# Dilated attention: exchanging the softmax statistics of two set layouts on chip, and scaling the second set on ScalarE

## The chip, the core and the metric

The kernel runs on one core of one Trainium2 chip. The metric is the device time of one execution in microseconds; the median of three runs before the change is 2357.65 us (2355.96 to 2360.38). Engines are named as the profile names them: PE is TensorE's matmul, PEld its weight load, DVE is VectorE, ACT is ScalarE, POOL is GpSimd, SP is SyncE, which only issues DMAs here.

## The reference, cut to what matters

Eight layers follow each other on 512 tokens of width 1024: a dilated attention ("dil"), a differential attention ("diff"), a recurrent mixer, cross attentions, MLPs and a sliding-window attention, each with a norm before and after. The change lies in the first one. For each of 16 heads there are three groups of queries, keys and values with (window, dilation) of (128, 1), (512, 4) and (2048, 16); each group has its own softmax over its own keys, and the three outputs are mixed by a softmax over the groups' log-denominators:

```python
    outs, lses = [], []
    for g, (window, dil) in enumerate(DIL_GROUPS):
        sl = slice(g * DIL_HEADS, (g + 1) * DIL_HEADS)
        o, lse = dilated_window_attention(q[:, :, sl], k[:, :, sl], v[:, :, sl], window, dil)
        outs.append(o)
        lses.append(lse)
    alpha = jax.nn.softmax(jnp.stack(lses, axis=0), axis=0)
    o = jnp.sum(alpha[..., None] * jnp.stack(outs, axis=0), axis=0)
    y = o.reshape(B, S, DIL_WIDTH).astype(h.dtype) * jax.nn.silu(gate)
    return y @ w_out
```

That mixing is the same as one softmax over the scores of all three groups together, for each query.

## The kernel before, in words

Matrix products in fp32 are made of three products of split operands (`mm3`, L364 to L372): an ACT instruction rounds a weight half to `whi` (L443), a DVE instruction takes the rest `wlo` (L444), and each pair of operands takes three matmuls (L370, L371, L372). A projection of 128 columns over 512 tokens (`unit`, L395) is 24 such matmuls into a PSUM tile `pj`.

The dilated stage (`dil`, L817) goes through eight pairs of heads (hp). For each pair it projects queries and keys of the three groups (`proj`, two units of 24 matmuls for each group), rotates them on DVE (L601) and POOL (L603), and lays them out as `qk` by DMAs of 32 partitions (L614, on the SP queue). While hp is projected, PE is also given the attention of the pair before: `plan` (L921) puts 18 steps of the generator `attend` (L830) into a list, and `fm` calls the next step between the matmuls of a unit, after its third and its sixth of eight pairs (`self.cuts = 3, 6`) and at its end. Six units with three calls each take the 18 steps of one pair. For the last pair (hp 7) two steps are taken at each call (`self.rate = 2`, L941).

The steps of one pair:

- Steps 0 to 3: scores of set 0 (group 0, queries in an order where partition p of tile i belongs to one block of 128 tokens), and their softmax part: a DVE instruction takes mask, scale and the negative maximum (L632), an ACT instruction the exponential with its sum (L634). Unnormalised weights go to `pa`, maximum and sum to `st[0]` [128 partitions, 4 tiles, 2 heads, 2 values].
- Steps 4 to 6: the same for set 1 (groups 1 and 2 share one softmax of 256 columns, tokens sorted by their residue mod 4) into `pb` and `st[1]`.
- Still in step 6: `merge(st)` (L953) and the scaling of `pa` and `pb` (L870).
- Steps 7 to 12 do nothing (`for _ in range(7): yield`, L872).
- Steps 13 to 17: `turn` transposes `pa` and `pb` on PE (L886), copies the result from PSUM to `PT` on ACT (L279) and DVE (L277), and `weigh` multiplies by the values (L900) into one PSUM tile `pv`; the first `turn` is that of `pa`.

In `merge` each set needs the other set's maximum and sum of the same query, which lies in another partition and another tile: query (partition 32 n + l, tile m) of one set is (partition 32 m + l, tile n) of the other. Before the change each `st` is written to a DRAM tile `ds` by one DMA (L960 for set 0, L961 for set 1) and read back in the other layout by four DMAs each (L965 into `ot[1]`, L966 into `ot[0]`), ten DMAs for each pair of heads on the SP queue. Then for each set nine small instructions on tiles of 8 columns form the factor `f` (DVE L973 to L975, ACT exponential L976, DVE L977 to L981), and 16 DVE instructions of up to 128x256 scale the weights (L870).

The order of each engine's queue is not the order of the source: the framework sorts the instructions when the kernel is built, giving each engine the earliest instruction of the source whose operands it reckons ready by then. On the chip each queue is then worked off strictly in that order, an instruction waits where its operands are late, and all behind it wait too. SP's queue holds the weight loads (L301), the `qk` moves (L614) and the ten DMAs of `merge`.

Of the kernel before, what the change touches and what calls it, by code (L numbers as in the profile page):

```python
# [12 lines left out]
F32 = mybir.dt.float32  # L13
F32R = mybir.dt.float32r
I32 = mybir.dt.int32
AF = mybir.ActivationFunctionType
ALU = mybir.AluOpType
# [3 lines left out]
S = 512  # L21
# [192 lines left out]
class Prog:  # L214
# [602 lines left out]
    def dil(self):  # L817
        nc = self.nc
        y = []
        self.v_phase("dil")  # L820
        with self.vg, self.pool("rt_dil") as rp, self.pool("dl") as p:
# [3 lines left out]
            v, gates, qk, sm = {}, self.gates, {}, {}  # L825
# [4 lines left out]
            def attend(hp):  # L830
                pa, pb = (p.tile([P, NT, 2, 256], F32, tag="p", name=n, bufs=2) for n in ("pa", "pb"))
                st = [self.sm.tile([P, 4, 2, 2], F32, tag=f"st{s}", name=f"st{s}", bufs=2) for s in range(2)]
                q0, q1, q2 = (qk.pop((hp, g)) for g in range(3))
                for i in range(NT):
                    lo = 0 if i else P
# [29 lines left out]
                f = self.merge(st)  # L865
                for s, pp in enumerate((pa, pb)):
                    for i in range(NT):
                        for h in range(2):
                            lo = P if s == 0 and i == 0 else 0
                            nc.vector.tensor_scalar(out=pp[:, i, h, lo:256], in0=pp[:, i, h, lo:256],  # L870
                                                    scalar1=f[s][:, i, h:h + 1], scalar2=None, op0=ALU.mult)
                for _ in range(7):  # L872
                    yield
                o = self.ps("pv")
# [46 lines left out]
            def plan(hp):  # L921

                it = attend(hp)

                def step(n):
                    next(it, None)
                    if n == 6 and hp:
                        gated(hp - 1)

                self.steps_between += [partial(step, n) for n in range(18)]  # L930
# [22 lines left out]
    def merge(self, st):  # L953

        nc = self.nc

        d = [self.dr.tile([S, 4], F32, tag=f"ds{s}", name=f"ds{s}", bufs=2) for s in range(2)]
        ot = [self.sm.tile([P, 4, 2, 2], F32, tag=f"ot{s}", name=f"ot{s}", bufs=2) for s in range(2)]
        st2, ot2 = ([t.rearrange("p i h c -> p i (h c)") for t in z] for z in (st, ot))
        nc.sync.dma_start(out=d[0].rearrange("(p i) c -> p i c", i=4), in_=st2[0])  # L960
        nc.sync.dma_start(out=d[1].rearrange("(r p) c -> p r c", r=4), in_=st2[1])  # L961
        of0, of1 = d[0].rearrange("(r l i) c -> i l r c", r=4, i=4), d[1].rearrange("(r i l) c -> r l i c", r=4, i=4)
        for n in range(4):
            ns = slice(32 * n, 32 * (n + 1))
            nc.sync.dma_start(out=ot2[1][ns], in_=of0[n])  # L965
            nc.sync.dma_start(out=ot2[0][ns], in_=of1[n])  # L966
        res = []
        for s in range(2):
            a, b = st[s], ot[s]
            e = self.sm.tile([P, 2, 4, 2], F32, tag="me", name="me", bufs=2)  # L970
            n = self.sm.tile([P, 4, 2], F32, tag="mn", name="mn", bufs=2)
            f = self.sm.tile([P, 4, 2], F32, tag=f"mf{s}", name=f"mf{s}", bufs=2)
            nc.vector.tensor_tensor(out=n, in0=a[:, :, :, 0], in1=b[:, :, :, 0], op=ALU.min)  # L973
            nc.vector.tensor_tensor(out=e[:, 0], in0=n, in1=a[:, :, :, 0], op=ALU.subtract)
            nc.vector.tensor_tensor(out=e[:, 1], in0=n, in1=b[:, :, :, 0], op=ALU.subtract)  # L975
            nc.scalar.activation(out=e, in_=e, func=AF.Exp)  # L976
            nc.vector.tensor_tensor(out=n, in0=e[:, 0], in1=a[:, :, :, 1], op=ALU.mult)  # L977
            nc.vector.tensor_tensor(out=f, in0=e[:, 1], in1=b[:, :, :, 1], op=ALU.mult)
            nc.vector.tensor_tensor(out=n, in0=n, in1=f, op=ALU.add)
            nc.vector.reciprocal(out=n, in_=n)  # L980
            nc.vector.tensor_tensor(out=f, in0=e[:, 0], in1=n, op=ALU.mult)  # L981
            res.append(f)
        return res
# [819 lines left out]
```

## Time and profile before

| What | Value |
|---|---|
| Median of three runs | 2357.65 us |
| The profiled execution's own time | 2357.28 us |
| Its span, first to last instruction | 2355.5 us |
| Mean granted TensorE clock | 0.997 of 2.4 GHz |
| Busy: PE, PEld | 2297.0 us (98%), 1872.4 us (79%) |
| Busy: DVE, ACT, POOL | 1429.9 us (61%), 1090.3 us (46%), 745.8 us (32%) |

The busy time of an engine is the union of its instructions' times; where it is short of the span, the engine was idle. The profile's views name for each idle stretch the releaser, what ended it. A timeline row merges neighbouring instructions of one form and shows in brackets the idle time in front of it. Attention of the dilated stage runs from about 209 to 610 us; its windows here are 195 to 640 us.

### The profile page before, as it was taken

The numbers are of one execution on the slowest core, as the hardware profiler recorded it, in microseconds if no ns is written. First come the engines' busy times: TensorE is split into PE (matmuls) and PEld (weight loads), VectorE is DVE, ScalarE is ACT, GpSimd is POOL, SyncE is SP. The second block draws the span as 40 slices with busy tenths as digits, with TensorE's granted clock in tenths as the row PEclk, the third lists the DMA queues.
The fourth block names the chain that finished last, engine by engine and source line by source line (L and its number), as shares of the span: only waits on it lengthen the run. The fifth ranks groups of instructions, "written<-read, shape, count | busy, mean of one in ns | idle before, by whom it ended". The sixth has DMA issues, their size and how long they took to land.

```text
span 2355.5 us, 33109 instructions
## 1 busy us (share of the span) xinstructions
PE 2297.0 (98%) x12168; PEld 1872.4 (79%) x12168; DVE 1429.9 (61%) x2458; ACT 1090.3 (46%) x2145; POOL 745.8 (32%) x799
## 2 busy tenths in 40 slices
PE   7999999999999999999999999999999999999998
PEld 6887777767788877878898888887966988888887
DVE  7664665666565555765655544468777744644476
ACT  4443333334344444544444454457456533544464
POOL 5962211211122222100300276671211200577640
PEclk9999999999999999999999999999999999999999
DMA  6335443333332222222442355556332332455555
GB/s 232 130 122 154 118 119 93 108 97 82 123 117 90 90 81 93 84 72 73 133 162 72 108 179 197 197 178 215 133 99 89 127 126 72 144 189 191 195 204 168
DMA packets 115874, 309.51 MB, mean 131 GB/s; under 512 B 28940, under 2 KB 35116, under 8 KB 115712
## 3 DMA queue, kind: packets, MB, share of 16 engines
q1 hardware_dynamic: 114912, 305.46, 39.2%
q0 software_dynamic: 800, 1.94, 0.3%
q8 instruction: 96, 1.57, 0.3%
q14 instruction: 66, 0.54, 0.1%
HBM read 253.72 MB, written 33.69 MB: 122 GB/s over the span
## 4 chain that ended last, share of the span: by engine, by line
PE 60%; DVE 4%; POOL 3%; ACT 2%; issue 2%; DMA 1%; SPq 0%; POOLq 0%; DVEq 0%; ACTq 0%
PE pj L370 13%; PE pj L371 13%; PE pj L372 13%; PE sc L370 3%; PE sc L371 3%; PE sc L372 3%; DVE wlo L444 1%; PE pv L370 1%; PE pv L372 1%; PE pv L371 1%; PE sc L1659 1%; PE sc L1024 1%; DVE h L521 1%; POOL quad L354 1%; PE pt L491 1%
## 5 line engine op out<-in xcount | busy, mean ns | idle before, releaser
L444 DVE TENSOR_TENSOR wlo<-raw,whi 128x1024 fp32r<-128x1024 f32 x348 | 445.3, 1286 | 329.6 <-ACT whi L443 317.2
L370 PE MATMUL pj<-uh,whi 128*128 128x512 f32 (+1 forms) x1424 | 561.9, 395 | 0.2 <-ACT ho L1350 0.2
L372 PE MATMUL pj<-uh,wlo 128*128 128x512 f32 (+1 forms) x1424 | 553.7, 389 | 2.1 <-DVE wlo L444 2.1
L371 PE MATMUL pj<-ul,whi 128*128 128x512 f32 (+1 forms) x1424 | 554.2, 389 | 0.0
L443 ACT ACTIVATE whi<-raw 128x1024 fp32r<-128x1024 f32 x348 | 365.7, 1057 | 394.1 <-PE pj L371 162.3
L354 POOL TENSOR_TENSOR quad<-quad 128x256 f32<-128x256 f32 x352 | 347.0, 1022 | 83.0 <-DVE wlo L444 37.9
L370 PEld LDWEIGHTS pj<-uh,whi 128*128 128x128 f32 x1424 | 268.0, 188 | 71.2 <-issue 15.9
L372 PEld LDWEIGHTS pj<-uh,wlo 128*128 128x128 f32 x1424 | 268.0, 188 | 60.1 <-issue 4.0
L371 PEld LDWEIGHTS pj<-ul,whi 128*128 128x128 f32 x1424 | 268.7, 189 | 54.2 <-issue 4.8
L603 POOL TENSOR_TENSOR ro<-rt 128x512 f32<-128x512 f32 x74 | 127.5, 1735 | 534.9 <-DVE rt L601 366.5
L466 POOL TENSOR_SCALAR rs<-ss 128x1 f32<-128x1 f32 x32 | 23.9, 747 | 540.6 <-ACT bq L512 540.3
L444 DVE TENSOR_TENSOR wlo<-quad,whi 128x1024 fp32r<-128x1024 f32 x90 | 124.8, 1390 | 75.7 <-ACT whi L443 75.6
L370 PE MATMUL sc<-whi,yh 128*128 128x512 f32 x384 | 151.3, 394 | 2.9 <-DVE acc L1524 2.9
L371 PE MATMUL sc<-wlo,yh 128*128 128x512 f32 x384 | 150.8, 393 | 1.0 <-DVE wlo L444 1.0
L372 PE MATMUL sc<-whi,yl 128*128 128x512 f32 x384 | 149.9, 391 | 0.0
L370 PE MATMUL pj<-whi,yh 128*128 128x512 f32 x360 | 141.9, 394 | 0.0
L371 PE MATMUL pj<-wlo,yh 128*128 128x512 f32 x360 | 141.0, 392 | 0.7 <-DVE wlo L444 0.5
L372 PE MATMUL pj<-whi,yl 128*128 128x512 f32 x360 | 140.9, 391 | 0.0
L443 ACT ACTIVATE whi<-quad 128x1024 fp32r<-128x1024 f32 x90 | 95.0, 1059 | 85.6 <-PE pj L371 35.8
L370 PEld LDWEIGHTS sc<-whi,yh 128*128 128x128 f32 x384 | 72.1, 188 | 21.3 <-ACT whi L443 2.0
L371 PEld LDWEIGHTS sc<-wlo,yh 128*128 128x128 f32 x384 | 72.1, 188 | 17.0 <-DVE wlo L444 2.3
L372 PEld LDWEIGHTS sc<-whi,yl 128*128 128x128 f32 x384 | 72.1, 188 | 14.8 <-DVE yl L444 0.2
(418 smaller groups left out, 4398.3 us busy)
## 6 DMA issues: line engine op xcount, KB each, us to landing
raw<-in_ws_dram SPq DMA_DIRECT2D x300, 512.0 KB, 3.7
quad<-in_ws_dram SPq DMA_DIRECT2D x88, 512.0 KB, 6.2
T<-quad SPq DMA_DIRECT2D x48, 512.0 KB, 3.0
raw<-T SPq DMA_DIRECT2D x48, 512.0 KB, 4.1
qk<-ro SPq DMA_DIRECT2D x256, 64.0 KB, 2.0
vd<-vo SPq DMA_DIRECT2D x24, 256.0 KB, 3.9
gpre<-in_gains_dram SPq DMA_DIRECT2D x8, 512.0 KB, 5.5
v<-vd SPq DMA_DIRECT2D x8, 512.0 KB, 4.3
```

Source lines behind the costliest of these rows:

```text
L354: self.nc.gpsimd.tensor_tensor(out=out[:, cs], in0=x[:, cs], in1=y[:, cs], op=ALU.subtract)
L370: self.nc.tensor.matmul(ps, lhsT=ah, rhs=bh, start=first and k == 0, stop=False, **kw)
L371: self.nc.tensor.matmul(ps, lhsT=ah, rhs=bl, start=False, stop=False, **kw)
L372: self.nc.tensor.matmul(ps, lhsT=al, rhs=bh, start=False, stop=last and k == n - 1, **kw)
L443: self.nc.scalar.activation(out=dst[0], in_=src, func=AF.Copy)
L444: self.nc.vector.tensor_sub(out=dst[1], in0=src, in1=dst[0].bitcast(F32))
L466: nc.gpsimd.tensor_scalar(out=r[:, 0:1], in0=ss[:, 0:1], scalar1=ss[:, 1:2], scalar2=EPS, op0=ALU.add, op1=ALU.add)
L491: nc.tensor.transpose(pt[:, k * P:(k + 1) * P], b[:, (4 * g + k) * P:(4 * g + k + 1) * P], self.ident)
L521: nc.vector.scalar_tensor_tensor(out=h, in0=b, scalar=r, in1=h, op0=ALU.mult, op1=ALU.add)
L603: nc.gpsimd.tensor_tensor(out=o, in0=t[0], in1=t[1], op=op)
L1024: nc.tensor.matmul(ps[:, :n], lhsT=q[hs, 0, i * P:n], rhs=q[hs, 1, :n], start=True, stop=True)
L1659: nc.tensor.matmul(ps[e][:, hp * 256 + lo:(hp + 1) * 256], lhsT=q[hs, hp, i * P:(i + 1) * P], rhs=kd[hs, g, (i - 1) * P + lo:(i + 1) * P], ...
```

## The change

The statistics no longer go to DRAM. For each set, 16 copies of 32 partitions by 4 values write `ot` from the other set's `st`: those into `ot[0]` (from `st[1]`) on ACT, those into `ot[1]` (from `st[0]`) on DVE (`copy` is an ACT activation with Copy for "s", a DVE copy for "v"). The scaling of `pb` becomes eight ACT activations with the factor as the scale operand; that of `pa` stays on DVE.

```diff
                     for i in range(NT):
                         for h in range(2):
                             lo = P if s == 0 and i == 0 else 0
-                            nc.vector.tensor_scalar(out=pp[:, i, h, lo:256], in0=pp[:, i, h, lo:256],
-                                                    scalar1=f[s][:, i, h:h + 1], scalar2=None, op0=ALU.mult)
+                            if s:
+                                nc.scalar.activation(out=pp[:, i, h], in_=pp[:, i, h], func=AF.Copy, scale=f[s][:, i, h:h + 1])
+                            else:
+                                nc.vector.tensor_scalar(out=pp[:, i, h, lo:256], in0=pp[:, i, h, lo:256],
+                                                        scalar1=f[s][:, i, h:h + 1], scalar2=None, op0=ALU.mult)
...
-        d = [self.dr.tile([S, 4], F32, tag=f"ds{s}", name=f"ds{s}", bufs=2) for s in range(2)]
         ot = [self.sm.tile([P, 4, 2, 2], F32, tag=f"ot{s}", name=f"ot{s}", bufs=2) for s in range(2)]
-        st2, ot2 = ([t.rearrange("p i h c -> p i (h c)") for t in z] for z in (st, ot))
-        nc.sync.dma_start(out=d[0].rearrange("(p i) c -> p i c", i=4), in_=st2[0])
-        nc.sync.dma_start(out=d[1].rearrange("(r p) c -> p r c", r=4), in_=st2[1])
-        of0, of1 = d[0].rearrange("(r l i) c -> i l r c", r=4, i=4), d[1].rearrange("(r i l) c -> r l i c", r=4, i=4)
-        for n in range(4):
-            ns = slice(32 * n, 32 * (n + 1))
-            nc.sync.dma_start(out=ot2[1][ns], in_=of0[n])
-            nc.sync.dma_start(out=ot2[0][ns], in_=of1[n])
+        for s in range(2):
+            for n in range(4):
+                for m in range(4):
+                    self.copy(ot[s][32 * n:32 * (n + 1), m], st[1 - s][32 * m:32 * (m + 1), n], "v" if s else "s")
```

## Rows read from the trace of the kernel before

**Rows 1.** The page: busy time of the engines, and engines of the chain that ended last.

```profile
PE 2297.0 (98%) x12168; PEld 1872.4 (79%) x12168; DVE 1429.9 (61%) x2458; ACT 1090.3 (46%) x2145; POOL 745.8 (32%) x799
...
PE 60%; DVE 4%; POOL 3%; ACT 2%; issue 2%; DMA 1%; SPq 0%; POOLq 0%; DVEq 0%; ACTq 0%
```

**Rows 2.** Waits of PE, 195 to 640 us: total us, times, longest us.

```profile
PE pt L886 <- DVE pa L870: 13.5, 8, 2.5
PE sc L841 <- DVE st L632: 3.7, 6, 0.6
```

**Rows 3.** Engine busy time by stretch, 195 to 640 us (PE, PEld, DVE, ACT, POOL).

```profile
195.00:640.00 445.00, 427.61 (x2387) 321.42 (x2386) 267.84 (x714) 159.40 (x390) 87.50 (x56) 0.99 0.38 110
```

**Rows 4.** PE's timeline around one merge, 540 to 562 us: start, us, instruction, idle before.

```profile
540.70 0.95 PE L857 MATMUL sc<-qk 64*128 64x128 f32 x8
541.58 0.50 PE L371 MATMUL pj<-ul,whi 128*128 128x512 f32 x1
...
544.22 0.39 PE L370 MATMUL pj<-uh,whi 128*128 128x512 f32 x1
...
544.90 0.39 PE L370 MATMUL pj<-uh,whi 128*128 128x512 f32 x1
...
554.42 0.39 PE L370 MATMUL pj<-uh,whi 128*128 128x512 f32 x1
556.58 0.79 PE L886 MATMUL pt<-ident,pa 128*128 128x128 f32 x3 [1.77 <-DVE pa L870]
557.12 0.49 PE L371 MATMUL pj<-ul,whi 128*128 128x512 f32 x1
...
558.44 0.48 PE L371 MATMUL pj<-ul,whi 128*128 128x512 f32 x1
```

**Rows 5.** DVE's timeline, same merge.

```profile
542.14 0.08 DVE L632 DVE_READ_ACCUMULATOR2_ANT st<- 128x1 f32 x1
544.49 0.69 DVE L601 TENSOR_TENSOR rt<-pj,cos 128x512 f32<-128x512 f32 x1 [2.27 <-PE pj L372]
...
551.92 0.30 DVE L973 TENSOR_TENSOR mn<-st,ot 128x8 f32<-128x8 f32 x2 [0.77 <-DMA ot<-ds]
...
554.18 1.28 DVE L977 TENSOR_TENSOR mn<-me,st 128x8 f32<-128x8 f32 x1
...
556.05 0.28 DVE L981 TENSOR_TENSOR mf<-me,mn 128x8 f32<-128x8 f32 x2
556.25 2.05 DVE L870 TENSOR_SCALAR pa<-pa,mf 128x128 f32<-128x128 f32 x8
```

**Rows 6.** SP's, ACT's and POOL's timelines, same merge.

```profile
544.68 0.53 SPq L961 DMA_DIRECT2D ds<-st  x1
...
547.31 1.74 SPq L966 DMA_DIRECT2D ot<-ds  x4
...
542.82 0.19 ACT L634 ACTIVATION_READ_ACCUMULATOR pb<-pb,st 128x1 f32 x1
...
553.00 0.37 ACT L976 ACTIVATE me<-me 128x16 f32<-128x16 f32 x2 [2.26 <-DVE me L975]
...
552.95 2.48 POOL L603 TENSOR_TENSOR ro<-rt 128x512 f32<-128x512 f32 x1 [0.98 <-DVE rt L601]
```

**Rows 7.** Timelines of ACT, DVE and PE around the last pair's merge, 588 to 606 us.

```profile
588.72 0.18 ACT L634 ACTIVATION_READ_ACCUMULATOR pb<-pb,st 128x1 f32 x1
...
596.62 0.30 DVE L973 TENSOR_TENSOR mn<-st,ot 128x8 f32<-128x8 f32 x2 [3.77 <-DMA ot<-ds]
...
598.11 0.28 DVE L981 TENSOR_TENSOR mf<-me,mn 128x8 f32<-128x8 f32 x2
...
596.76 0.39 PE L370 MATMUL pj<-whi,yh 128*128 128x512 f32 x1
598.65 0.52 PE L886 MATMUL pt<-ident,pa 128*128 128x128 f32 x2 [1.50 <-DVE pa L870]
...
604.87 1.09 PE L886 MATMUL pt<-ident,pb 128*128 128x128 f32 x8
605.89 0.88 PE L900 MATMUL pv<-PT,v 128*64 128x128 f32 x12
```

**Rows 8.** Clock by stretch: times as in group 3, then granted clock, DMA share, GB/s.

```profile
398.00:400.00 2.00, 2.00 (x10) 1.56 (x9) 2.00 (x9) 0.41 (x1) 0.00 (x0) 0.52 0.35 95
400.00:402.00 2.00, 2.00 (x9) 1.23 (x7) 2.00 (x6) 0.50 (x2) 0.00 (x0) 0.63 0.64 234
...
452.00:454.00 2.00, 2.00 (x11) 1.67 (x10) 2.00 (x9) 0.52 (x1) 0.00 (x0) 0.67 0.49 130
454.00:456.00 2.00, 2.00 (x8) 1.16 (x6) 2.00 (x6) 0.46 (x2) 0.00 (x0) 0.50 0.60 227
```

**Rows 9.** Prices, from groups by line and form: mean ns, or min/median/max ns.

```profile
L1667 ACT ACTIVATE ses<-ses 128x4 f32<-128x4 f32 x16 | 3.1, 196 | 0.4 <-DVE ses L1666 0.2
L1067 ACT ACTIVATE on<-pv,dsc 128x128 f32<-128x128 f32 x32 | 9.1, 369 | 14.3 <-POOL dsc L1065 14.3
L634 ACT ACTIVATE pb<-pb,st 128x256 f32<-128x256 f32 x64 | 32.0, 501 | 33.4 <-DVE st L632 33.4
L870 DVE TENSOR_SCALAR pb<-pb,mf x64: 342/345/352, 243.2 to 602.1; 128x256 f32<-128x256 f32 x64
L974 DVE TENSOR_TENSOR me<-mn,st x16: 149/157/166, 239.8 to 597.0; 128x8 f32<-128x8 f32 x16
```

**Rows 10.** PE's timeline after the second pair's merge, and ACT's after the first.

```profile
293.20 0.79 PE L886 MATMUL pt<-ident,pa 128*128 128x128 f32 x3 [1.59 <-DVE pa L870]
...
299.38 0.88 PE L886 MATMUL pt<-ident,pb 128*128 128x128 f32 x6
...
243.57 0.60 ACT L279 ACTIVATE PT<-pt 128x512 f32<-128x512 f32 x1 [3.14 <-PE pt L886]
```

## The prediction

> **What bounds the kernel now.** I read the page first: PE is busy for 2297.0 of 2355.5 us and holds 60% of the chain that ended last, where DVE has 4% and the DMAs 1% [rows 1]. So a shorter path on another engine is worth only what PE now waits for. The second view is PE's waits in the dilated attention: 13.5 us in eight waits go to one cause, the first transpose (L886) of a pair of heads, which waits for DVE's scaling of `pa` (L870); six waits of 3.7 us go to score matmuls that wait for DVE's maxima [rows 2]. PE's whole idle time there is 445.00 - 427.61 = 17.4 us, so these two are all of it [rows 3], and no wait of PE there names a DMA. Over the rest of the kernel PE is idle for 2355.5 - 2297.0 - 17.4 = 41.1 us, which the change does not touch.
>
> The third view, the timelines around one merge, shows why `pa` is late. The last sum of `st[1]` is there at 542.82 + 0.19 = 543.0 us [rows 6]. The write to DRAM is issued at 544.68, the four reads of it start only at 547.31, when that write has landed [rows 6], and DVE's first merge instruction runs at 551.92, with the arrival of `ot` as releaser [rows 5]: 8.9 us from the last sum, for the way out and back. The merge then takes until 556.33, stretched by other work in DVE's queue and by one instruction of 1.28 us (L977) that ends where POOL's L603 ends (552.95 + 2.48 = 555.43) [rows 5, 6]. PE has issued a matmul at 554.42, would issue the next 0.23 us later (three take 544.90 - 544.22 = 0.68), and goes on only at 556.58 [rows 4].
>
> The fourth view is the granted clock. It is full but for two places, 398 to 402 and 452 to 456 us, where it falls to between 0.50 and 0.67 of 2.4 GHz, so to 1.2 GHz for most of these stretches [rows 8]. Both lie just behind one of the eight waits; behind the other six no such fall is seen.
>
> **The change, part by part.** *The ten DMAs of each merge go*, 80 over the eight pairs, with their waits in SP's queue. The path from the last sum to the factor was 8.9 us to the first merge instruction and 4.4 us through it [rows 5, 6]. In its place come 16 copies on ACT, of which the last four need the last tile of `st[1]`; the copies from `st[0]` on DVE can be done long before. The nearest ACT row, 128x4 at 196 ns [rows 9], makes four 0.8 us, and all sixteen 3.2 us if none is done ahead: the copies end at 543.8, at worst 546.2. The merge, undisturbed as for the last pair, takes 598.11 + 0.28 - 596.62 = 1.8 us [rows 7], as stretched as here 4.4 us: `f` is there at 545.6, at worst 550.6. Eight scalings of `pa` take 2.05 us [rows 5], so all of `pa` is ready at 547.7 to 552.7. PE wants the first of them at 554.65: a margin of 2 to 7 us. For the last pair, with less cover, the same sums give 588.9 + 0.8 + 1.8 + 2.1 = 593.6, at worst 598.6, where PE stops at 597.0 [rows 7] and needs a first piece alone; I count it as covered too. So the eight waits go: **-13.5 us** [rows 2].
>
> *The two falls of the clock go* if they come from those stops: 2.0 x (0.48 + 0.37) = 1.7 us for the first and 2.0 x (0.33 + 0.50) = 1.7 us for the second [rows 8]. Bounds are nothing and 3.4; I take **-3.4**, because both follow such a wait, and the stage shows no other fall.
>
> *Transposes mixed with matmuls.* Released one by one, eight transposes and three matmuls took 558.44 - 556.58 = 1.86 us [rows 4]; eight transposes in one block take 1.02 [rows 7], three matmuls 0.68, together 1.70. Eight times 0.16 gives **-1.3**. Lower bound nothing, if the new order mixes them as well.
>
> *16 copies on DVE for each pair.* The trace has no DVE copy of 32 partitions from SBUF. The nearest is a DVE instruction of 128x8, 157 ns long [rows 9], of which a pair takes 0.30 or less [rows 5], so overlapped about 0.08 each. They can stand anywhere between the softmax parts; DVE is busy for 267.8 of 445 us [rows 3], and what they could hold up is PE's six waits for DVE's maxima [rows 2]. One copy in front of each costs 6 x 0.157 = **+0.9**; the least is nothing (even less, as DVE also loses eight scalings of 0.35 us for each pair [rows 9]), the most, all 128 copies on the path, 128 x 0.157 = 20, from which the idle third of DVE keeps me far. I take the whole length and not the overlapped one, since these copies read other partitions than they write, which no row here does. The Trainium skill (VectorE: DVE Perf Modes, "Two Vector instructions with no wait between them") says that an instruction whose input starts in another group of 32 partitions than the last one's begins only when all before it have ended. By that the copies would not overlap and the term would be the 0.9 taken, by overlap 0.5; no run here shows which.
>
> *The scaling of `pb` on ACT.* The nearest ACT rows are 128x256 from SBUF with a per-partition operand, 501 ns, and 128x128 with a per-partition scale, 369 ns [rows 9]; I take 501, so eight are at most 4.0 us, against 8 x 0.345 = 2.8 us taken off DVE. They come after `f`, at 545.6 to 550.6, and end by 549.6 to 554.6, while the transposes of `pb` start 299.38 - 293.20 = 6.2 us after those of `pa` [rows 10]. ACT is busy for 159.4 of 445 us [rows 3]; copies and scalings add at most 8 x (3.2 + 4.0) = 58. What they may push back are weight halves (L443), needed a unit later. I cost this at **nothing**; the cover is the time between `f` and `pb`'s transposes, 10 us and more, and without it 4.0 us for each pair.
>
> *SP's queue* loses 80 issues of about 0.4 us and their waits [rows 6], with weight loads and `qk` moves behind them. No wait of PE in the stage names either [rows 2]: nothing.
>
> *Later stages* get their queues' order from the same reckoning at build, so it may shift; I take nothing and bound it by a tenth of the 41.1 us, 4 us each way.
>
> **The sum.** 2357.28 us of the profiled execution (span 2355.5) - 13.5 - 3.4 - 1.3 + 0.9 = **2340.0 us**. That execution stands 0.4 us under the median of 2357.65, too little to correct for.
>
> **The rivals.**
>
> *A part of the wait stays.* The small instructions of the merge remain behind other work in DVE's queue, as L973 to L981 stand between L601 and L444 now, and the first `pa` comes some tenths late, or the clock falls stay. With half of the 18.2 us gained: 2357.3 - 9.1 = 2348 us. For it: the merge stretched to 4.4 us here; against it: 2 us of margin even then. The Trainium skill (SBUF — State Buffer, section "Summary: rules for kernel authors" and the rules before it) has DVE copies within SBUF among the instructions that block POOL or are blocked by it for a whole instruction. The L977 row shows such a wait on POOL's L603 for another operation; a copy's is shown by no row. Chance 0.12.
>
> *The wait is only renamed (no change).* If the builder's reckoning puts the new copies so late that `f` still comes with the same units, PE stops eight times as now: 2357 us. It needs the on-chip chain to lose its 2 to 7 us margin. The removal of 80 tiny DMAs and of DVE time alone would give nothing, since no PE wait names them. Chance 0.10.
>
> *ACT becomes the late engine (slower).* ACT works its queue in order. If the eight scalings of `pb` stand in it just ahead of the copy of the first transposes (`PT`, L279), PE's weighing waits for them: 8 pairs x 4.0 us = 32 us, while the 18.2 us are gained: 2357.3 - 18.2 + 32 = 2371 us. It decides from the point where `f` comes less than 4.0 us before the first transposes. For it: ACT had only 3.14 us free before the first `PT` copy when the factor came late [rows 10]. Against it: `f` should come 4 us (550.6 to 554.65) to 9 us before. Chance 0.06.
>
> **How the numbers follow.** The forecast, 2335 to 2347 us, has a chance of 0.72: its low end takes the rest of the 3.7 us as well and drops the copies' 0.9, with PE kept as busy as it can be. The 8-in-10 range adds the partial case up to 2351: 2335 to 2351. A difference of 0.2% (4.7 us) is about the least that a measurement of this kernel can tell from none. Faster by more than that: 0.72 + 0.11 = 0.83; within: 0.11; slower: 0.06.
>
> **What would show it.** In the new profile: no wait of PE's transposes for `pa` above a few tenths, granted clock full between 195 and 640 us, PE idle there under 7 us; DVE's first merge instruction within 2 to 4 us after the last sum of `st[1]` instead of 8.9; ACT copies of 32x4 near 196 ns and scalings near 500 ns; eight merges' transposes in unbroken blocks of seven or eight. The prediction is wrong if PE waits as long for another releaser (ACT's `pb` or `PT`, score matmuls for DVE), or if PE's idle time outside this stretch grows by more than 4 us.

## The result, and the profile after

The changed kernel takes 2338.01 us (median of 4 runs, 2335.89 to 2339.04), against 2357.67 us before in the same comparison: a ratio of 0.9914, 95% interval 0.9897 to 0.9932. The forecast was 2340.0 us, so faster than before. The profiled execution took 2335.89 us, 21.4 us less than the one before; the sum had 17.3 us. Medians of further runs come from comparisons in which the kernel before stood at 2361 to 2362 us, so across comparisons only ratios are compared below. The changed kernel, run once more there, gave 0.9905 (0.9892 to 0.9919).

The page's busy times, to be held against [rows 1]:

```profile
PE 2287.8 (98%) x12168; PEld 1871.5 (80%) x12168; DVE 1432.2 (61%) x2522; ACT 1140.8 (49%) x2337; POOL 744.9 (32%) x799
```

ACT has 50 us more to do, DVE the same as before, PE 9.2 us less although its 12168 instructions are the same. That last number is already a hint: PE did not only wait less.

The waits of PE in the window of [rows 2] and the busy times of the window of [rows 3] after the change:

```profile
PE sc L841 <- DVE st L632: 3.7, 6, 0.6
PE pt L889 <- DVE pa L873: 1.9, 1, 1.9
PE pt L491 <- DVE bu L483: 0.9, 1, 0.9
```

```profile
195.00:640.00 445.00, 438.42 (x2541) 339.65 (x2540) 289.12 (x803) 221.26 (x602) 97.81 (x69) 1.00 0.38 116
```

Of the eight stops of 13.5 us in all, seven are gone and one of 1.9 us stays. The score matmuls' waits for DVE's maxima are what they were, 3.7 us; below they are called waits for score banks, since such a matmul writes a PSUM bank that DVE's instruction L632 has to read first. The row of L491 belongs to the next stage, which comes into the window because the dilated stage ends sooner. The later layers start earlier by the whole gain and move no more than 1 us against each other (the first scores of the next attention begin at 654.3 us instead of 676.4, the last output is issued at 2331.1 instead of 2352.4).

PE around the merge of the seventh pair, the place of [rows 4]:

```profile
520.76 0.94 PE L857 MATMUL sc<-qk 64*128 64x128 f32 x8
...
533.82 1.03 PE L889 MATMUL pt<-ident,pa 128*128 128x128 f32 x8
...
536.08 0.82 PE L889 MATMUL pt<-ident,pa 128*128 128x128 f32 x6
```

No idle time stands in front of the transposes, and they come as one block of eight and one of six. DVE and ACT at the same merge, the place of [rows 5, 6]:

```profile
522.89 0.19 ACT L634 ACTIVATION_READ_ACCUMULATOR pb<-pb,st 128x1 f32 x1
523.10 1.49 ACT L279 ACTIVATE ot<-st 32x4 f32<-32x4 f32 x7
...
527.16 3.31 ACT L871 ACTIVATE pb<-pb,mf 128x256 f32<-128x256 f32 x8 [1.70 <-DVE mf L979]
...
524.62 0.24 DVE L971 TENSOR_TENSOR mn<-st,ot 128x8 f32<-128x8 f32 x2 [2.33 <-ACT ot L279]
...
526.78 0.28 DVE L873 TENSOR_SCALAR pa<-pa,mf 128x128 f32<-128x128 f32 x1
...
527.05 1.85 DVE L873 TENSOR_SCALAR pa<-pa,mf 128x128 f32<-128x128 f32 x7
```

From the last sum (523.08) to the first merge instruction 1.5 us pass, where it was 8.9 us; all of `pa` is scaled by 528.9, 4.9 us ahead of the first transpose.

The last pair is the exception. ACT, DVE and PE there, the place of [rows 7], and the clock behind it, as in [rows 8]:

```profile
567.18 0.18 ACT L634 ACTIVATION_READ_ACCUMULATOR pb<-pb,st 128x1 f32 x1
567.39 1.70 ACT L279 ACTIVATE ot<-st 32x4 f32<-32x4 f32 x8
569.12 1.06 ACT L443 ACTIVATE whi<-raw 128x1024 fp32r<-128x1024 f32 x1
570.08 0.30 ACT L974 ACTIVATE me<-me 128x16 f32<-128x16 f32 x2
...
570.21 1.23 DVE L444 TENSOR_TENSOR wlo<-raw,whi 128x1024 fp32r<-128x1024 f32 x1 [0.48 <-ACT whi L443]
...
571.74 0.68 DVE L622 SCALAR_TENSOR_TENSOR gate<-gate,pj 128x512 f32<-128x512 f32 x1
...
573.11 0.33 PE L889 MATMUL pt<-ident,pa 128*128 128x128 f32 x1 [1.89 <-DVE pa L873]
```

```profile
574.00:576.00 2.00, 2.00 (x9) 1.52 (x8) 0.90 (x4) 2.00 (x7) 0.00 (x0) 0.50 0.00 0
576.00:578.00 2.00, 2.00 (x8) 1.62 (x7) 0.69 (x1) 0.95 (x3) 0.00 (x0) 0.65 0.00 0
```

Eight ACT copies stand behind the last sum, then the exponential of the merge waits behind a weight half, and DVE's part of the merge behind the other weight half and a gate. PE stops for 1.9 us, and the clock is at its lower level for most of the next 4 us.

### The profile page after: what moved, and what is told of

The parts are those of the page before. It is cut to its first block, busy times and chain, and to the rows that moved or that the text cites. A ratio compares the mean times of both kernels' runs of the same rounds, so it can differ in the third digit from the quotient of the medians.

```text
span 2334.1 us, 33247 instructions
## 1 busy us (share of the span) xinstructions
PE 2287.8 (98%) x12168; PEld 1871.5 (80%) x12168; DVE 1432.2 (61%) x2522; ACT 1140.8 (49%) x2337; POOL 744.9 (32%) x799
## 3 DMA queue, kind: packets, MB, share of 16 engines
q0 software_dynamic: 800, 1.94, 0.3%
## 4 chain that ended last, share of the span: by engine, by line
PE 61%; DVE 5%; POOL 2%; ACT 2%; issue 2%; DMA 1%; SPq 0%; POOLq 0%; DVEq 0%; ACTq 0%
PE pj L370 13%; PE pj L371 13%; PE pj L372 13%; PE sc L371 3%; PE sc L370 3%; PE sc L372 3%; DVE wlo L444 1%; PE pv L370 1%; PE pv L371 1%; PE pv L372 1%; PE sc L1657 1%; PE sc L1022 1%; DVE h L521 1%; PE pt L491 1%; POOL rs L469 1%
## 5 line engine op out<-in xcount | busy, mean ns | idle before, releaser
L444 DVE TENSOR_TENSOR wlo<-raw,whi 128x1024 fp32r<-128x1024 f32 x348 | 452.4, 1308 | 301.0 <-ACT whi L443 284.9
L370 PEld LDWEIGHTS pj<-uh,whi 128*128 128x128 f32 x1424 | 267.6, 188 | 72.2 <-issue 17.3
L603 POOL TENSOR_TENSOR ro<-rt 128x512 f32<-128x512 f32 x74 | 127.4, 1737 | 512.4 <-DVE rt L601 415.2
L444 DVE TENSOR_TENSOR wlo<-quad,whi 128x1024 fp32r<-128x1024 f32 x90 | 125.3, 1395 | 76.2 <-ACT whi L443 76.1
```

What stands on the lines that cost most here:

```text
L370: self.nc.tensor.matmul(ps, lhsT=ah, rhs=bh, start=first and k == 0, stop=False, **kw)
L444: self.nc.vector.tensor_sub(out=dst[1], in0=src, in1=dst[0].bitcast(F32))
L603: nc.gpsimd.tensor_tensor(out=o, in0=t[0], in1=t[1], op=op)
```

## The experiments

Three theories were put against each other. The *late factor*: PE stopped, and got its transposes split up, because the factor came late; any way to have it earlier gives the same gain. The rivals: the 80 small DMAs cost time in themselves, or DVE's load did. In some of the waits shown, the row of the next stage (L491) is left out.

**Each half of the change alone.** First the exchange on chip, with `pb` scaled on DVE as before:

```diff
-                            if s:
-                                nc.scalar.activation(out=pp[:, i, h], in_=pp[:, i, h], func=AF.Copy, scale=f[s][:, i, h:h + 1])
-                            else:
-                                nc.vector.tensor_scalar(out=pp[:, i, h, lo:256], in0=pp[:, i, h, lo:256],
-                                                        scalar1=f[s][:, i, h:h + 1], scalar2=None, op0=ALU.mult)
+                            nc.vector.tensor_scalar(out=pp[:, i, h, lo:256], in0=pp[:, i, h, lo:256],
+                                                    scalar1=f[s][:, i, h:h + 1], scalar2=None, op0=ALU.mult)
```

> The exchange on chip, with the second set scaled on DVE as before. Theory (the late factor: PE stops and has its transposes mixed among projections because the statistics go through DRAM): pa is scaled first on DVE, so it is as early as in the changed kernel; seven of the eight stops go, the last pair's of about 1.9 us stays, and the time is 2336 to 2342 us, within 0.2% of the changed kernel's 2338.0. Rival (taking the eight scalings of 345 ns off DVE does part of it): the time stands at least 5 us above the changed kernel's, 2343 us or more, with PE waits for pa left in several pairs.

Measured: 2338.83 us, ratio 0.9905 (0.9892 to 0.9919), the changed kernel's own value. Its waits of PE in the window:

```profile
PE sc L841 <- DVE st L632: 3.7, 6, 0.6
PE pt L886 <- DVE pa L870: 1.9, 1, 1.9
```

They are the changed kernel's, the last pair's stop among them. With the factor early, it makes no difference here which engine scales `pb`. Then the other half, the scaling on ACT with the statistics still through DRAM (the first hunk of the change alone):

> The second set scaled on ACT, the statistics still through DRAM. Theory (late factor): pa still waits for the way through DRAM, so eight stops of about 1.7 us and their mixed transposes stay; 2355 to 2360 us, no change from 2357.7. Rival (DVE's load): at least 5 us faster, 2352 us or less. Second rival (the scalings on ACT stand ahead of the first PT copy): slower than 2362 us, with PE waiting for PT.

Measured: 2353.06 us, ratio 0.9968 (0.9955 to 0.998). "No change" was wrong: against the 2361.04 us of the kernel before in this comparison it is 8 us faster, as the first rival had it ("at least 5 us"). The waits were as the theory has them, the time was not:

```profile
PE pt L889 <- DVE pa L873: 13.5, 8, 2.0
PE sc L841 <- DVE st L632: 3.7, 6, 0.6
```

All eight stops are there with the same 13.5 us. What differs is the order: of the second `turn`'s six transposes, which before came in two threes with weighing and projections between them, all come in one block. One pair before, and two here:

```profile
507.21 0.54 PE L886 MATMUL pt<-ident,pa 128*128 128x128 f32 x3
507.67 0.43 PE L900 MATMUL pv<-PT,v 128*64 128x128 f32 x2
...
509.32 0.49 PE L886 MATMUL pt<-ident,pa 128*128 128x128 f32 x3
```

```profile
498.35 0.79 PE L889 MATMUL pt<-ident,pa 128*128 128x128 f32 x3 [1.80 <-DVE pa L873]
...
502.15 0.82 PE L889 MATMUL pt<-ident,pa 128*128 128x128 f32 x6
...
549.80 0.79 PE L889 MATMUL pt<-ident,pa 128*128 128x128 f32 x3 [1.85 <-DVE pa L873]
```

The period from pair to pair is 549.80 - 498.35 = 51.45 us here with a stop of 1.85 us, so 49.6 us without it. Before it was 345.12 - 293.20 = 51.92 us with 1.62 us, so 50.3 us. The 0.7 us between them is PE time that no wait shows. So DVE's load was worth something after all, not through a wait. With eight scalings off DVE, its copy of the first transposes begins 500.58 - 498.35 = 2.2 us after the first of them, where it was 508.31 - 504.57 = 3.7 us; that the order made at the build splits less for this reason is inferred, not tried by itself.

Over the seven periods from the first pair's transposes to the last's, this execution gains 4.1 us beside stops and falls of the clock. At the last pair's transposes it is 598.65 - 591.58 = 7.1 us ahead of the one before: those 4.1 us, 1.3 us that it was ahead when the stage began (its first scores at 206.69 us instead of 208.00), and 1.7 us of one fall of the clock less. Of the 7.1 us, 3.7 are left at the end of the span, because the clock falls twice more behind that place (at 592 to 598 us after a stop of 1.8 us, and at 1124 to 1130 us), at 1.7 us each. So the order accounts for some 4 of the 8 us; the rest of the difference in the medians stays open.

**The DMAs kept, the factor earlier.** The kernel before with `merge` moved from step 6 to step 4, transposes still at step 13:

```diff
                     if i % 2:
                         yield
-                        yield
+                        if i == 1:
+                            yield
...
                     if r == 1:
                         yield
-                        yield
...
-                for _ in range(7):
+                for _ in range(9):
```

> The kernel before, with all its DMAs and DVE scalings, but merge moved from step 6 to step 4 of the 18 (about 3.6 us earlier against the transposes, which stay at step 13). Theory (late factor): the way through DRAM is then covered too; the stops of the first seven pairs go, the transposes come in unbroken blocks of eight, and the time falls to 2336 to 2346 us though every DMA is still there. Rival (the 80 small DMAs or SP's queue cost time in themselves): little is gained, 2352 us or more.

Measured: 2351.4 us, ratio 0.9961 (0.9948 to 0.9973): between the two, and the theory's range missed. PE's waits say why:

```profile
PE pt L886 <- DVE PT L277: 8.9, 6, 2.4
PE sc L841 <- DVE st L632: 3.7, 6, 0.6
PE pt L886 <- DVE pa L870: 1.6, 1, 1.6
```

The stops for `pa` are gone but for the last pair's, and the eight transposes come in a block; a new stop stands right behind them, at the copy of their result on DVE. DVE's timeline:

```profile
281.17 0.24 DVE L973 TENSOR_TENSOR mn<-st,ot 128x8 f32<-128x8 f32 x2 [0.71 <-DMA ot<-ds]
...
284.83 2.19 DVE L870 TENSOR_SCALAR pb<-pb,mf 128x256 f32<-128x256 f32 x8
286.93 0.68 DVE L601 TENSOR_TENSOR rt<-pj,sin 128x512 f32<-128x512 f32 x1
...
288.73 3.63 DVE L444 TENSOR_TENSOR wlo<-raw,whi 128x1024 fp32r<-128x1024 f32 x2
292.28 0.68 DVE L277 COPY PT<-pt 128x512 f32<-128x512 f32 x1
```

The way through DRAM still takes 6.8 us from the last sum (274.4, from ACT's row) to the first merge instruction, and DVE comes to the copy only at 292.28, 3.3 us after the transposes began: it works off merge, sixteen scalings, three rotations and two weight halves without a pause. So the stop moved to the next late thing. The same kernel with `pb` scaled on ACT takes 2.2 us of that queue away:

> Statistics through DRAM, merge two steps earlier as in the run before it (e3), and the second set scaled on ACT. Theory (late factor, and in e3 DVE's queue, which worked off pb's scalings and the delayed rotations before the PT copy): DVE is 2.2 us for each pair less behind, the six stops for PT of 0.9 to 2.4 us shrink below 0.5 us each, and the time comes to 0.991 to 0.994 of the kernel before with all 80 DMAs in place. Rival (the DMAs cost time in themselves): it stays at e3's 0.996.

Measured: 2338.72 us, ratio 0.9904 (0.9891 to 0.9918), with all 80 DMAs in place the changed kernel's time. PE's waits are 3.7 us for score banks, 1.6 us once for `pa` and one of 0.3 us for `PT`:

```profile
PE sc L841 <- DVE st L632: 3.7, 6, 0.6
PE pt L889 <- DVE pa L873: 1.6, 1, 1.6
...
PE pt L889 <- DVE PT L277: 0.3, 1, 0.3
```

The ratio is a little below its expected 0.991 to 0.994. So the rival falls: the 80 DMAs in themselves cost nothing that these runs can tell. What they cost was the time at which the factor came, and the same gain is to be had without an exchange on chip. The closest comparison comes below: with the same steps and the exchange on chip the ratio is 0.9892 (0.9878 to 0.9905), and the intervals overlap.

**How much margin.** The changed kernel with fewer empty steps, so that the transposes are wanted earlier (`range(5)`, then `range(3)` in place of `range(7)`).

> The changed kernel with five empty steps instead of seven, so that the transposes come two steps, about 3.6 us, earlier. The factor's margin in the changed kernel is 533.82 - 527.05 less one piece, about 5 to 6.5 us before the first transpose; theory (margin): still covered, no stop in the first seven pairs, 2334 to 2342 us. Rival (the margin is used up by ACT's scalings of pb and the PT copies): stops of 1 us or more return, 2345 us or more.

Measured: 2335.87 us, ratio 0.9894 (0.9879 to 0.9909). No stop came back in the first seven pairs, as the margin of 4.9 us has it, and something else went:

```profile
PE pt L889 <- DVE pa L873: 1.6, 1, 1.6
...
PE sc L841 <- DVE st L632: 0.6, 1, 0.6
```

The waits for score banks fall from 3.7 to 0.6 us. A likely reason, not tried by itself, is that the last weighing now stands two steps away from the next pair's first scores, so that DVE frees the banks in time. The period falls from 49.2 to 48.5 us (533.82 - 484.63 in the changed kernel, 527.34 - 478.80 here). The time does not show it as clearly, since the interval overlaps the changed kernel's; this execution loses 3.4 us to a fall of the clock at 972 to 980 us, in a later stage, which the changed kernel's two executions do not have.

> The changed kernel with three empty steps instead of seven: the transposes are wanted four steps, about 7.3 us, earlier than in the changed kernel, at 533.82 - 7.3 = 526.5 in its times, where the first pa is scaled only at 527.1. Theory (the factor's margin sets it): in seven pairs the transposes are mixed among projections again and stops of 0.5 to 1.5 us return though no DMA does; 8 to 16 us slower than the changed kernel, 0.994 to 0.998 of the kernel before. Rival (the gain came from the 80 DMAs being gone): as fast as the changed kernel, 0.991.

Measured: 2341.49 us, ratio 0.9915 (0.9901 to 0.9928), as fast as the changed kernel, where 0.994 to 0.998 was expected. By its time alone the rival's figure came true; but the stops did come back:

```profile
PE pt L889 <- DVE pa L873: 6.1, 8, 1.6
...
PE sc L841 <- DVE st L632: 0.6, 1, 0.6
```

They are of 0.63 to 0.66 us in the seven pairs, inside the 0.5 to 1.5 us expected. The fault was in the yardstick: this run also has the 0.65 us for each pair that the run before gained, and against that run its ratio is 0.0021 higher, 5 us, with periods of 529.36 - 479.86 = 49.50 against 48.54 us. Of that 0.96 us, 0.65 is the stop and 0.3 the split-up transposes of the first `turn`. So the margin is real: it ends between two and four steps, and the run that keeps all 80 DMAs speaks against the rival.

**Both early, and DVE alone.** `merge` two steps earlier in the changed kernel (the edit of the DRAM run), transposes at step 13:

> The changed kernel with merge two steps earlier, transposes at the same step 13. Theory: the first seven pairs had margin already and gain nothing; only the last pair's stop of 1.9 us and the clock's fall behind it (1.7 us) can go: 0.989 to 0.991 of the kernel before. Rival (still more of the time hangs on the factor): 0.988 or less.

Measured: 2336.68 us, ratio 0.9892 (0.9878 to 0.9905). The first seven pairs are unchanged (no stop for `pa`, 3.7 us for score banks), the last stop went from 1.9 to 1.5 us, and no fall of the clock follows it in this execution. The interval reaches up to the changed kernel's 0.9905 below. Then with transposes at step 11 (`range(7)` again):

> The changed kernel with merge two steps earlier and transposes at step 11, so that margin is as in the changed kernel and the weighing of a pair ends two steps before the next pair's scores, as in e4. Theory: e4's gain over the changed kernel came from PE's waits for score banks (3.7 us to 0.6 us) and comes again, with the last pair's stop smaller: 0.987 to 0.989 of the kernel before, the fastest. Rival (e4's 0.9894 was a clock fall less, no more): 0.990 to 0.991.

Measured: **2334.1 us, ratio 0.9883 (0.987 to 0.9897)**, the lowest of all. PE's waits in the window:

```profile
PE pt L889 <- DVE pa L873: 1.2, 1, 1.2
...
PE sc L841 <- DVE st L632: 0.6, 1, 0.6
```

PE is idle for 445.00 - 442.23 = 2.8 us of the window. Against the changed kernel in its comparison beside the next run (0.9905) the intervals overlap; its profiled span, 2331.1 us, is 2.4 to 3.0 us below that kernel's two, 2334.1 and 2333.5 us.

> The changed kernel once more, on the chip and in the rounds of the run beside it. Theory and rival alike: 0.990 to 0.992 of the kernel before; PE's idle time within 195 to 640 us 6 to 7 us, one stop of about 1.9 us in the last pair.

Measured: 2337.84 us, ratio 0.9905 (0.9892 to 0.9919); idle 445.00 - 438.41 = 6.6 us, the stop 1.9 us. Beside it, all 32 copies of a pair on DVE in the fastest kernel:

```diff
-                    self.copy(ot[s][32 * n:32 * (n + 1), m], st[1 - s][32 * m:32 * (m + 1), n], "v" if s else "s")
+                    self.copy(ot[s][32 * n:32 * (n + 1), m], st[1 - s][32 * m:32 * (m + 1), n], "v")
```

> As e10 (merge two steps earlier, transposes at step 11), with all 32 copies of a pair on DVE and none on ACT. In e10 eight ACT copies stand between the last sum and the first merge instruction of the last pair, 1.70 us. Theory (the last pair's stop hangs on those copies): on DVE four or eight of them take 0.17 to 0.19 us each, 0.7 to 1.5 us, without ACT's weight half in between, and the last stop of 1.25 us shrinks to under 0.8 us; 0.987 to 0.989 of the kernel before, within noise of e10. Rival (DVE is the fuller engine, and 16 more copies of 0.17 us for each pair come in front of its maxima): PE's waits for score banks grow above 2 us in total and the time rises above 0.990.

Measured: 2343.51 us, ratio 0.9924 (0.9911 to 0.9936), 0.0041 higher than with the copies shared out, almost 10 us. The theory's stop in the last pair did go, but the rival has the time:

```profile
PE pt L889 <- DVE PT L277: 6.1, 7, 0.9
PE sc L858 <- DVE st L632: 2.2, 7, 0.3
PE sc L841 <- DVE st L632: 0.6, 1, 0.6
```

PE waits for DVE's copy of the transposes (0.87 us in each of seven pairs) and for the maxima (0.3 us). DVE is busy for 306.95 us of the window, 282.89 in the run before the copies were moved; as in the DRAM run, its queue is too full at the place where PE needs it.

## Why the prediction was right

*The wait that ends last* was read right. The stops for `pa` went in the seven pairs for which 2 to 7 us of margin were forecast, measured 4.9 us. The first merge instruction comes 1.5 us after the last sum (2 to 4 us forecast); copies take 203 ns on ACT (196 taken) and scalings 496 ns (501 taken). The prediction's claim that taking away the DMAs by itself gives nothing is borne out by the run that keeps them and has the gain. The other half of that claim, that DVE's time alone gives nothing because no wait of PE names it, was wrong: the scaling alone gave a ratio of 0.9968, through the order of PE's instructions and not through a wait.

*The last pair* was the step that failed. It was counted as covered, from four copies behind the last sum and an undisturbed merge of 1.8 us. Eight copies stood there (1.70 us), the merge took from 569.12 to 573.13 with a weight half and a gate in its way, and PE wanted `pa` at 571.1, 3.7 us after the last sum where it had been 8.1 us: the builder had moved those transposes ahead as well. 11.6 us of stops went, not 13.5.

*The clock.* Two falls of 1.7 us each before, one of the same size after, so 1.7 us gained and not 3.4. The fall after stands again behind the last pair's stop, of 1.89 to 1.94 us, in both executions of the changed kernel and in that of the exchange alone. With `merge` or the transposes moved in the on-chip kernel, or both, that stop takes 1.2 to 1.6 us and no fall follows in the stage. Length alone doesn't decide: before, stops of 1.62 us at 345 and at 397 us went without a fall and with one, and in the run with the scaling alone one of 1.78 us had a fall and one of 1.85 us had none. Nor does every fall stand behind a stop. In six of the ten later runs the clock is at 0.50 for part of 972 to 988 us, in a stage that the change does not touch, at a cost of 1.7 us in one and 3.4 us in five, and no wait of PE in the ten microseconds before is longer than 0.3 us; the same code runs there at 1.00 in the other executions. So which falls an execution has varies without a stop to account for it, and that a stop brings one on is likely but not shown. The forecast that both falls go with the stops of the first seven pairs came true. "Full but for two places" holds for the stage alone: at 18 to 24 us the kernel before has a third fall (0.80, 0.50, 0.85), but the stage begins at 208.0 us before and 207.7 after, so it has no part in the gain.

*The split transposes* were the term that was mis-sized: -1.3 us forecast, from 0.16 us for the first eight of each pair. Periods without their stops are 345.12 - 293.20 - 1.62 = 50.3 us before and 337.23 - 288.02 = 49.2 us after, so 1.1 us for this pair. Over the six periods between the first seven pairs, less stops and falls, it is 5.9 us, so about 1 us for each pair and some 7 us for the seven; the last pair's transposes are still split. PE's busy time bears it out: it fell by 9.2 us, of which 1.7 are the clock's and 7.5 are left. This is what carried the gain above the sum. The prediction looked at eight transposes and three matmuls, and not at the second `turn`: its threes with weighing between them are the larger part, 0.6 to 0.7 us by the run with the scaling alone, and the first `turn`'s 0.3 to 0.4 us. That such a split costs PE time is shown by the periods; how it does was not tried.

*DVE's copies* cost nothing on the path: PE's waits for its maxima are 3.7 us as before, +0.9 us forecast. They are not overlapped, as the prediction took it:

```profile
510.34 1.48 DVE L277 COPY ot<-st 32x4 f32<-32x4 f32 x8
```

One copy takes 0.16 us, so the others start (1.48 - 0.16) / 7 = 0.19 us apart, where DVE's L972 and L973 of the merge start 0.08 us apart with the same length. That agrees with the Trainium skill (VectorE: DVE Perf Modes, "Two Vector instructions with no wait between them"), by which each of these copies, if they stand in the order of the source, starts only when all before it have finished.

The terms together, with nothing for the copies: 11.6 + 1.7 + 7 = 20.3 us of the 21.4 us measured, -17.3 us forecast; the other 1.1 us is not accounted for. The gains from stops and clock were forecast 3.6 us too large, the one from the order some 6 us too small, and the copies' cost 0.9 us too large. That the time came so near is in part luck.

*The rivals.* A part of the wait stays: so it was for the last pair, as this rival has it, with the merge behind other work in DVE's queue (L444, L622) and a fall of the clock behind the stop; the seven other pairs kept their margin. Wait only renamed: not so in this kernel, but the DRAM run shows a stop that moves, with DVE's `PT` copy in the place of `pa`. ACT as the late engine: its scalings begin at 527.16 and end by 530.5, ahead of the first `PT` copy; it never came near.

## What to carry to other kernels

Where an engine at 98% waits for a small value that goes around, ask by when the value is needed, not what its way costs: the same gain came from a way on chip, or from the same slow way begun two steps earlier with the consumer's queue lightened. Look at the order of the bound engine's instructions beside its waits; splitting a run of small products among others cost here more than half as much as the stops that went, and no wait row shows it. And after removing one wait, place the next step again: moving the transposes two steps ahead, into the margin that the change had made, took away most of another wait.

## What the hardware showed that was not expected

- ACT's small copies do not overlap: eight of 32x4 take 1.70 us, so they start (1.70 - 0.20) / 7 = 0.21 us apart at a length of 203 ns. Eight scalings of 128x256 take 3.31 us and start 0.40 us apart at a length of 496 ns, so they do.
- A DVE copy of four columns can be blocked for more than a microsecond. With all copies on DVE, four of them take 1.77 us, and the longest single one 1239 ns against a median of 161 ns, while POOL works on its rotation (L603):

```profile
526.65 1.77 DVE L277 COPY ot<-st 32x4 f32<-32x4 f32 x4
```

```profile
526.75 1.29 POOL L603 TENSOR_TENSOR ro<-rt 128x512 f32<-128x512 f32 x1 [15.38 <-DVE rt L601]
```

```profile
L277 DVE COPY ot<-st x256: 152/161/1239, 213.0 to 577.7; 32x4 f32<-32x4 f32 x128
```

  In the changed kernel the longest of 128 such copies took 168 ns; none of them ran beside a rotation on POOL. The Trainium skill (SBUF — State Buffer, "Summary: rules for kernel authors") says that while DVE runs in a two-port mode, and by the rules before it a copy within SBUF can, DVE and POOL shut each other out: the one that issues second waits until the first is done. The trace agrees on the wait: the four copies begin 0.1 us before POOL's instruction, and one of them takes about as long as that instruction, 1.29 us. Which mode the copies ran in it does not show.
- Some stops of PE of 1.6 to 2.5 us have a fall of the granted clock right behind them, to 0.50 (1.2 GHz) at its lowest, at a cost of 1.7 us, so about as much again as the stop. Seven of the eight stops of the run with the scaling alone are of 1.6 to 2.0 us, and two of them have one. Other falls have no such stop in front of them, as told above.
